# VectorE's order in a hybrid decoder trunk: residual adds ahead of waiting work, held banks later in the seventh part, values' low parts behind the softmax

## The chip, the cores and the metric

The kernel runs on one core of a Trainium2 chip. The metric is the time of one execution in microseconds (us). Its engines are named in the profile as PE (TensorE, matmuls), PEld (TensorE's weight loads, which overlap matmuls), DVE (VectorE), ACT (ScalarE), POOL (GpSimd) and SP (SyncE, which issues the loads).

## The reference

One sequence of 256 tokens with 2048 features goes through two layers. Layer 0 mixes tokens with a gated linear recurrence (RG-LRU), layer 1 with attention over 16 heads; each mixer is followed by an MLP with 8192 hidden features. All is float32.

```python
for i in range(DEPTH):                       # DEPTH = 2
    h = _rmsnorm(x, mix_norm[i])
    x = x + (_rglru_block(h, ...) if i % 2 == 0 else _dilated_attention_block(h, w_qkv, w_o))
    x = x + _mlp(_rmsnorm(x, mlp_norm[i]), mlp_w1[i], mlp_w2[i])
return _rmsnorm(x, final_norm)

def _mlp(h, w1, w2):                         # 2048 -> 8192 -> 2048
    return square(relu(h @ w1)) @ w2
```

## The kernel before

**Numbers in two halves.** Each operand of a matmul is split into a high part (rounded to `float32r`) and a low part, the rest. A product is then three matmuls: high by high, high by low, low by high. ScalarE rounds a weight tile of 128 x 2048 to its high part (`whi`, line 132) and VectorE subtracts to get the low part (`wlo`, line 136), one pair per tile that is loaded. The same split is made of the activations: `xT` is the scaled input turned round (line 218 its low half), `aT` the hidden features of the MLP, `sT` sums of them, `av` the values of the attention.

**Items and slots.** The whole program is a list of items. An item is TensorE's work on one weight tile. Around it the loop at the end writes the other engines' work in a fixed order, and each engine runs its own list strictly in that order: first the weight halves that are due (`before_unit`, two items ahead for `wlo`, three for `whi`), then the item itself, then all functions that were put down for this slot with `after(n, fn)` (n items later), then those put down with `at_end` (behind all others of the slot). Within a slot the functions of `after` stand in the order in which they were put down, but `att_p`, the transposes of a softmax, goes first.

**The residual.** It lies in four chunks `xc` of 512 features (`xc_68` to `xc_71` in the order's rows, chunk 0 to 3), each in two tiles of 128 tokens. When a product's bank in PSUM is complete, VectorE adds it to the residual: `add_x` (line 366) for plain products, `take` (line 686) in the MLPs. At the end of a stage `close_chunk` makes the function `done` for a chunk: it adds, takes square sums on ScalarE (line 270), and puts down `transpose_chunk` for the next slot, in which TensorE turns the chunk (line 242), ScalarE scales it into `xg` (245) and both make `xT` from it.

**The MLP.** It runs in eight parts, 0 to 7, of 1024 hidden features. In the parts 0 to 6 the second product is done for a pair of blocks by a scheme with seven products in place of eight (Strassen's, in Winograd's form): `b11`, `b21`, `t1`, `t2`, `b22`, `t3`, `t4`, once for the chunks 0 and 1 ("0" behind the name) and once for the chunks 2 and 3 ("1"). Between them lie eight items "w" of the first product of the part that follows. The order is a table:

```python
2: ("w", "b11 0", "t1 0", "w", "b21 0", "b22 0", "t2 0", "w", "t3 0", "w", "t4 0", "b11 1", "t1 1", "w",
    "b22 1", "t2 1", "w", "t3 1", "b21 1", "w", "w", "t4 1"),
HELD = {0: ("B", "T", "C"), 2: ("B",)}
```

Products gather in banks A, B, C and T. Those in `HELD` keep one of the four `acc` banks through the parts 0 to 6 and are added only in the seventh part (part 6). The others use the two `tr` banks in turn and are added right behind their product. The eight projections and the attention's scores use two `g` banks. In part 7 the second product is plain, and each chunk takes two `acc` banks.

**What follows an item "w".** `u_done` (line 592) scales it on VectorE into `uu`, ScalarE squares it and writes the high half of `aT`, and one slot later `u_low` (line 601) writes its low half on VectorE. Lines 612 to 625 make the sums `sT` from two such tiles; line 682 makes sums of weight tiles (`qT`).

**The attention.** Each head's scores go through `att_s`, `att_e` (exponentials, ScalarE, line 841), `att_n` (scaling, VectorE, lines 846 and 848, put down with `at_end`) and `att_p` (transposes, TensorE, line 853). `v_done` (lines 774 and 775) makes the two halves of the values `av` from two `acc` banks for four heads at a time.

Of the kernel before, what the change touches and what calls it, by code (L numbers as in the profile page):

```python
# [10 lines left out]
F32 = mybir.dt.float32  # L11
F32R = mybir.dt.float32r
AF = mybir.ActivationFunctionType
OP = mybir.AluOpType
# [55 lines left out]

HELD = {0: ("B", "T", "C"), 2: ("B",)}

TAKES = {"b11": 0, "b21": 0, "t1": 0, "t2": 0, "b22": 0, "t3": 0, "t4": 0}


@with_exitstack
def trunk(ctx: ExitStack, tc: tile.TileContext, a: dict, out: bass.AP):
    nc = tc.nc
# [14 lines left out]
    def form(load, make, source):  # L93

        units.append({"load": load, "make": make, "source": source})
        return len(units) - 1
# [69 lines left out]
    def item(u, fn, kind=None):  # L166
        items.append((u, fn, kind))

    later = {}
    now = [0]  # L170
# [20 lines left out]
    def after(n, fn, *args):  # L191
        later.setdefault(now[0] + n, []).append((fn, args))
# [3 lines left out]
    def at_end(fn, *args, **kwargs):  # L196

        ending.append((fn, args, kwargs))
# [15 lines left out]
    state = {}  # L214
# [5 lines left out]
    def new_xT(n):  # L220
        t = perm.tile([P, 4, 512], F32R, name=f"xT{n}")
        state["xT", n] = t
        return t
# [4 lines left out]
    def new_xg(n):  # L228
        if scope[0] in ("mlp", "end"):
            t = lru.tile([P, UW], F32, name=("q12", "q22")[n % 2])  # L230
            return t[:, 0:4 * S].rearrange("p (k s) -> p k s", k=4)
        return lru.tile([P, 4, S], F32, name="xg", bufs=2)
# [33 lines left out]
    def square_sum(n, ts=range(NT)):  # L266
        sq = state["ssq"]
        for t in ts:
            junk = perm.tile([P, 512], mybir.dt.bfloat16, name="junk")
            nc.scalar.activation(junk, xc[n][:, t, :], AF.Square, accum_out=sq[:, t, n:n + 1])  # L270

    def new_ssq():
        state["ssq"] = perm.tile([P, NT, NCH], F32, name="ssq", bufs=2)
# [64 lines left out]
    def three(bank, xh, xl, hi, lo, opens, closes, border):  # L338

        mm(bank, xh, in_turn(hi), opens, False)  # L340
        mm(bank, xh, in_turn(lo), False, False)
        cut = 256 if border else 512
        for at in range(0, 512, cut):
            mm(bank[:, at:at + cut], xl, in_turn(hi, at, cut), False, closes and at + cut == 512)
# [5 lines left out]
    def acc_tile():  # L350
        return psum.tile([P, 512], F32, name="acc", bufs=4)
# [12 lines left out]
    def add_x(n, acc):  # L364
        for t in range(NT):
            nc.vector.tensor_add(xc[n][:, t, :], xc[n][:, t, :], acc[t])

    def close_chunk(n, gname, rows):
        def done(acc):
            if n == 0:  # L370
                new_ssq()
            add_x(n, acc)
            if n < NCH - 1:
                square_sum(n)
            after(1, transpose_chunk, n, gname)
            if n == NCH - 1:
                after(1, square_sum, n)
                after(1, rstd_cols)
                if rows:
                    after(4, rstd_rows)  # L380
        return done

    def aT(j):
        return state["aT", j]
# [237 lines left out]
    def low_of_sums():  # L622
        if "low" in state:
            t, w = state.pop("low")
            nc.vector.tensor_sub(t[:, 4:8], w, t[:, 0:4].bitcast(F32))  # L625

    def standing(p, what):

        def get(k):
            if what[0] == "a":  # L630
                t, h = int(what[1]) - 1, int(what[2]) - 1
                x = aT(8 * (p % 2) + 4 * h + k)
                return x[:, t * 128:(t + 1) * 128], x[:, 256 + t * 128:256 + (t + 1) * 128]
            x = state["sT", p, k]
            return x[:, int(what[1])], x[:, 4 + int(what[1])]
        return get

    def plan_mlp(w1, w2, done):
# [26 lines left out]
        def plan_group(p, n0, last_group):  # L665


            q, bank = {}, held.setdefault(n0, {})
            ends = GROUPS[p + 1] < GROUPS[p]

            def fetch(name, h, n, tag):
                q[name] = (wts.tile([P, UW], F32, name="raw", bufs=RAW_BUFS) if tag == "raw"
                           else lru.tile([P, UW], F32, name=tag))
                nc.sync.dma_start(q[name], w2[((p // 2) * 4 + n0 + n) * 4 + (p % 2) * 2 + h])

            def add(to, a, b, by):
                if by == "dma":
                    nc.gpsimd.dma_start(q[to], q[b], accum_op=OP.add)
                    return
                if to not in q:  # L680
                    q[to] = lru.tile([P, UW], F32, name=to)
                nc.vector.tensor_add(q[to], q[a], q[b])  # L682

            def take(n, t, b, sign):
                x = xc[n0 + n][:, t, :]
                (nc.vector.tensor_add if sign > 0 else nc.vector.tensor_sub)(x, x, bank[b])  # L686

            def product(name, loads, source, what, b, first, takes):
                def load_all():
                    for l in loads:  # L690
                        fetch(*l)

                def make_all():
                    for m in SUMS.get(name, []):
                        add(*m)
                u = form(load_all, make_all, lambda: q[source])

                def run():
                    opens = first and (p == 0 or b not in HELD[n0])
                    if opens:  # L700
                        bank[b] = acc_tile() if b in HELD[n0] else psum.tile([P, 512], F32, name="tr", bufs=2)
                    hi, lo = split[u]
                    get = standing(p, what)
                    for k in range(4):
                        xh, xl = get(k)
                        s = slice(k * 512, (k + 1) * 512)
                        three(bank[b], xh, xl, hi[:, s], lo[:, s], opens and k == 0, k == 3,
                              state["border"] and k == 3)
                    for t in takes if ends or b not in HELD[n0] else ():
                        after(TAKES[name], take, *t)  # L710
                    if what == "s0" and last_group:
                        busy[0] = None
                    if what == "a11":
                        busy[0] = p
                item(u, run)

            table = (
                ("b11", [("b11", 0, 0, "raw")], "b11", "a11", "A", True, [(0, 0, "A", 1)]),
                ("b21", [("q21", 1, 0, "q21")], "q21", "a12", "B", True, [(0, 0, "B", 1)]),
                ("t1", [("q12", 0, 1, "q12")], "qT", "s3", *(  # L720
                    ("T", True, [(1, 1, "T", -1), (1, 0, "T", -1)]) if "T" in HELD[n0] else ("C", True, [(1, 1, "C", -1)]))),
                ("t2", [("q22", 1, 1, "q22")], "qT", "s1", "A", False, [(1, 0, "A", -1)]),
                ("b22", [], "q22", "s2", "C", "T" in HELD[n0], [(1, 0, "C", -1)]),
                ("t3", [], "q12", "s0", "A", False, [(1, 1, "A", -1)]),
                ("t4", [], "q21", "a22", "A", False, [(0, 1, "A", 1)]),
            )
            return {row[0]: (lambda row=row: product(*row)) for row in table}
# [29 lines left out]
    scale = HD ** -0.5  # L757
# [11 lines left out]
    def v_done(g, acc):  # L769
        v = lru.tile([P, 2, NT, 4, HD], F32R, name="av", bufs=2)  # L770
        att["v", g] = v
        for t in range(NT):
            col, x = state["rstd"][:, t:t + 1], acc[t].rearrange("p (h d) -> p h d", h=4)
            nc.scalar.activation(v[:, 0, t], x, AF.Copy, scale=col)
            nc.vector.scalar_tensor_tensor(v[:, 1, t], x, col, v[:, 0, t].bitcast(F32), op0=OP.mult, op1=OP.subtract)

    def qk_done(h, w, ps):
        y = lru.tile([P, S], F32, name="y", bufs=4)
# [287 lines left out]
    for n in range(NCH):  # L1066
        x = new_xg(n)
        t = new_xT(n)
# [18 lines left out]
        for what in order:  # L1087
            k = int(what[1])
            if what[0] == "w":
# [7 lines left out]
                                           op0=OP.mult, op1=OP.subtract)  # L1097
# [39 lines left out]
    for at, (u, fn, kind) in enumerate(items):  # L1137
        if u is None:
            fn()
            continue  # L1140
        before_unit(u)
        state["border"] = kind is None and at + 1 < len(items) and items[at + 1][2] == "w"
        fn()
        behind_unit(least[at] - 1)
        for f, args in sorted(later.pop(now[0], []), key=lambda e: e[0] is not att_p):
            f(*args)
        for f, args, kwargs in ending:
            f(*args, **kwargs)
        ending.clear()
        low_of_sums()  # L1150
        sums_of_tokens()
        if kind is None:
            sums_of_tokens()
        now[0] += 1
# [87 lines left out]
```

## Time and profile before

| | |
|---|---|
| time, median of 3 runs (lowest to highest) | 2021.68 us (2021.48 to 2022.02) |
| the profiled execution's own time | 2022.14 us |
| its span, first to last instruction | 2020.4 us |
| granted TensorE clock | 0.999 |
| busy: PE, PEld, DVE, ACT, POOL | 2006.2, 1876.2, 1724.6, 1293.7, 88.4 us |

A row of the order of time reads: start in us, length in us, engine, line, operation, output and input tiles, shape, count, and in brackets how long the engine stood idle before it and what ended that. A row of waits gives the engine and line that waited, on whom, the total in us, how often and the longest. A row of a group gives its count, busy time, mean ns of one, and idle time before. A row of windows gives the stretch, its length, the busy time of PE, PEld, DVE, ACT and POOL with instruction counts, the granted clock, the share of the DMA engines and GB/s.

Matmuls run at a regular step: a matmul of 512 columns starts 0.216 us after the one before, one of 256 columns 0.112.

### The profile page before, as it was taken

The numbers are of one execution on the slowest core, as the hardware profiler recorded it, in microseconds if no ns is written. First come the engines' busy times: TensorE is split into PE (matmuls) and PEld (weight loads), VectorE is DVE, ScalarE is ACT, GpSimd is POOL, SyncE is SP. The second block draws the span as 40 slices with busy tenths as digits, with TensorE's granted clock in tenths as the row PEclk, the third lists the DMA queues.
The fourth block names the chain that finished last, engine by engine and source line by source line (L and its number), as shares of the span: only waits on it lengthen the run. The fifth ranks groups of instructions, "written<-read, shape, count | busy, mean of one in ns | idle before, by whom it ended". The sixth has DMA issues, their size and how long they took to land.

```text
span 2020.4 us, 32932 instructions
## 1 busy us (share of the span) xinstructions
PE 2006.2 (99%) x13761; PEld 1876.2 (93%) x13761; DVE 1724.6 (85%) x1903; ACT 1293.7 (64%) x1420; POOL 88.4 (4%) x83
## 2 busy tenths in 40 slices
PE   9999999999999999999999999999999999999998
PEld 9999988999999999999889989889999999999997
DVE  7999865699999999998658959857999999999985
ACT  7878775566566666665657657656666666666664
POOL 0111110000000000000000000000000000000001
PEclk9999999999999999999999999999999999999999
DMA  8555565688787788777554555456787877887774
GB/s 310 204 195 201 183 229 190 246 252 250 258 284 264 230 292 270 248 238 255 197 214 175 186 188 179 176 193 245 250 250 264 283 265 228 297 270 248 233 260 153
DMA packets 68917, 472.54 MB, mean 234 GB/s; under 512 B 7584, under 2 KB 7712, under 8 KB 13472
## 3 DMA queue, kind: packets, MB, share of 16 engines
q1 hardware_dynamic: 60416, 411.18, 54.2%
q0 software_dynamic: 8064, 58.72, 14.6%
q8 instruction: 108, 1.77, 0.3%
q10 hardware_dynamic: 288, 0.52, 0.1%
q14 instruction: 41, 0.34, 0.0%
HBM read 409.58 MB, written 2.10 MB: 204 GB/s over the span
## 4 chain that ended last, share of the span: by engine, by line
PE 91%; DVE 6%; ACT 2%; issue 1%; DMA 0%; SPq 0%; DVEq 0%; ACTq 0%
PE acc L201 44%; PE g L201 29%; PE tr L201 17%; DVE wlo L136 3%; ACT whi L132 1%; DVE qT L682 1%; PE tr L242 0%; DVE xc L686 0%; DVE c L437 0%; PE tr L853 0%; DVE sT L625 0%; DVE uu L592 0%; DVE aT L601 0%; DMA par<-in_par 0%; DVE sw L612 0%
## 5 line engine op out<-in xcount | busy, mean ns | idle before, releaser
L132 ACT ACTIVATE whi<-raw 128x2048 fp32r<-128x2048 f32 (+1 forms) x309 | 568.9, 1845 | 317.1 <-PE acc L201 163.1
L136 DVE TENSOR_TENSOR wlo<-raw,whi 128x2048 fp32r<-128x2048 f32 (+1 forms) x309 | 678.1, 2197 | 96.7 <-ACT whi L132 96.3
L201 PE MATMUL g<-xT,whi 128*128 128x256 f32 x3649 | 617.1, 275 | 0.0
L201 PEld LDWEIGHTS g<-xT,whi 128*128 128x128 f32 x3649 | 553.9, 192 | 0.0
L201 PE MATMUL g<-xT,wlo 128*128 128x256 f32 x1824 | 503.0, 276 | 0.6 <-DVE wlo L136 0.4
L201 PE MATMUL acc<-xT,whi 128*128 128x256 f32 (+1 forms) x2212 | 456.3, 301 | 0.3 <-ACT whi L132 0.3
L201 PE MATMUL acc<-xT,wlo 128*128 128x256 f32 x1360 | 374.1, 275 | 0.6 <-DVE wlo L136 0.6
L201 PEld LDWEIGHTS acc<-xT,whi 128*128 128x128 f32 x2212 | 356.3, 192 | 14.4 <-ACT whi L132 1.2
L201 PEld LDWEIGHTS g<-xT,wlo 128*128 128x128 f32 x1824 | 350.1, 192 | 2.2 <-DVE wlo L136 1.1
L201 PE MATMUL acc<-whi,aT 128*128 128x512 f32 (+1 forms) x1086 | 322.9, 374 | 0.0
L136 DVE TENSOR_TENSOR wlo<-q,whi 128x2048 fp32r<-128x2048 f32 x112 | 255.8, 2284 | 23.5 <-ACT whi L132 23.2
L132 ACT ACTIVATE whi<-q 128x2048 fp32r<-128x2048 f32 x112 | 214.4, 1915 | 79.3 <-PE g L201 53.3
L201 PEld LDWEIGHTS acc<-xT,wlo 128*128 128x128 f32 x1360 | 261.9, 193 | 1.4 <-DVE wlo L136 1.3
L201 PEld LDWEIGHTS acc<-whi,aT 128*128 128x128 f32 x1086 | 204.0, 189 | 27.6
L201 PE MATMUL tr<-whi,sT 128*128 128x512 f32 (+1 forms) x728 | 212.8, 364 | 0.9
L201 PE MATMUL acc<-wlo,aT 128*128 128x512 f32 (+1 forms) x536 | 200.8, 376 | 0.0
L132 ACT ACTIVATE whi<-qT 128x2048 fp32r<-128x2048 f32 x56 | 107.6, 1922 | 127.5 <-PE g L201 93.0
L201 PEld LDWEIGHTS tr<-whi,sT 128*128 128x128 f32 x728 | 137.7, 189 | 24.1 <-issue 6.1
L201 PE MATMUL tr<-whi,aT 128*128 128x512 f32 (+1 forms) x462 | 140.3, 373 | 0.0
L136 DVE TENSOR_TENSOR wlo<-qT,whi 128x2048 fp32r<-128x2048 f32 x56 | 127.9, 2284 | 1.3 <-ACT whi L132 1.3
L201 PE MATMUL tr<-wlo,sT 128*128 128x512 f32 x336 | 127.3, 379 | 0.0
L201 PEld LDWEIGHTS acc<-wlo,aT 128*128 128x128 f32 x536 | 101.1, 189 | 13.2
(170 smaller groups left out, 2147.5 us busy)
## 6 DMA issues: line engine op xcount, KB each, us to landing
raw<-in_w SPq DMA_DIRECT2D x172, 1024.0 KB, 6.9
q<-in_w SPq DMA_DIRECT2D x84, 1024.0 KB, 8.0
raw<-in_w_in SPq DMA_DIRECT2D x35, 1024.0 KB, 4.8
raw<-in_w_qk SPq DMA_DIRECT2D x32, 1024.0 KB, 4.8
q<-q POOLq DMA_DIRECT2D x28, 1024.0 KB, 12.2
q<-qT POOLq DMA_DIRECT2D x28, 1024.0 KB, 7.5
raw<-in_w_out SPq DMA_DIRECT2D x20, 1024.0 KB, 4.8
raw<-in_w_v SPq DMA_DIRECT2D x16, 1024.0 KB, 4.8
```

The source lines that it names most:

```text
L132: nc.scalar.activation(split[i][0][:, s], r, AF.Copy)
L136: nc.vector.tensor_sub(split[i][1][:, s], r, split[i][0][:, s].bitcast(F32))
L201: nc.tensor.matmul(o, l, r, start=start, stop=stop, skip_group_check=True)
L682: nc.vector.tensor_add(q[to], q[a], q[b])
```

## The change

Three edits in the code that sets the order. `take` and `closed` (the new name of the function that `close_chunk` returns) now go first in their slot, like `att_p`. The adds of the held banks in part 6 are put down 12, 12, 18 and 3 items after their product, where it was 0; the 18 reaches the second item of part 7. `v_done` puts its two pairs of instructions down with `at_end`, so that they stand behind the softmax's scaling where both fall in one slot.

```diff
-TAKES = {"b11": 0, "b21": 0, "t1": 0, "t2": 0, "b22": 0, "t3": 0, "t4": 0}
+ENDS = {"t1 0": 12, "b21 0": 12, "b22 0": 18, "b21 1": 3}
...
     def close_chunk(n, gname, rows):
-        def done(acc):
+        def closed(acc):
...
-        return done
+        return closed
...
-                        after(TAKES[name], take, *t)
+                        after(ENDS[f"{name} {n0 // 2}"] if b in HELD[n0] else 0, take, *t)
...
         for t in range(NT):
-            col, x = state["rstd"][:, t:t + 1], acc[t].rearrange("p (h d) -> p h d", h=4)
-            nc.scalar.activation(v[:, 0, t], x, AF.Copy, scale=col)
-            nc.vector.scalar_tensor_tensor(v[:, 1, t], x, col, v[:, 0, t].bitcast(F32), op0=OP.mult, op1=OP.subtract)
+            at_end(v_part, v, t, state["rstd"][:, t:t + 1], acc[t].rearrange("p (h d) -> p h d", h=4))
+
+    def v_part(v, t, col, x):
+        nc.scalar.activation(v[:, 0, t], x, AF.Copy, scale=col)
+        nc.vector.scalar_tensor_tensor(v[:, 1, t], x, col, v[:, 0, t].bitcast(F32), op0=OP.mult, op1=OP.subtract)
...
-        for f, args in sorted(later.pop(now[0], []), key=lambda e: e[0] is not att_p):
+        for f, args in sorted(later.pop(now[0], []), key=lambda e: e[0].__name__ not in ("att_p", "take", "closed")):
```

TensorE, GpSimd and SyncE run the same instructions in the same order as before. ScalarE's order differs in two places, where two square sums (line 270) of chunk 1 now stand ahead of `xg` and `xT` of chunk 0. The rest is VectorE's. The function that closes a chunk at the end of the last MLP (`final_done`) keeps its name and its place. New lines behind the diff's first edit are numbered 2 higher where the function lies behind `v_done`.

VectorE in part 0 of the first MLP, behind the items `t3 0` (first pair of rows that moves) and `t4 0` (second pair); `aT` is `u_low`'s, `xc` with `tr` a `take`. Before:

```order
L682 TENSOR_TENSOR qT<-raw,q_4749 128x2048
L601 TENSOR_TENSOR aT_4808<-uu,aT_4808 128x256
L686 TENSOR_TENSOR xc_69<-xc_69,tr 128x512
L136 TENSOR_TENSOR wlo<-raw,whi 128x2048
L592 SCALAR_TENSOR_TENSOR uu<-g,rstdB 128x256
L136 TENSOR_TENSOR wlo<-qT,whi 128x2048
L601 TENSOR_TENSOR aT_4888<-uu,aT_4888 128x256
L686 TENSOR_TENSOR xc_68<-xc_68,tr 128x512
L136 TENSOR_TENSOR wlo<-raw,whi 128x2048
```

VectorE at the same place now:

```order
L682 TENSOR_TENSOR qT<-raw,q_4749 128x2048
L686 TENSOR_TENSOR xc_69<-xc_69,tr 128x512
L601 TENSOR_TENSOR aT_4808<-uu,aT_4808 128x256
L136 TENSOR_TENSOR wlo<-raw,whi 128x2048
L592 SCALAR_TENSOR_TENSOR uu<-g,rstdB 128x256
L136 TENSOR_TENSOR wlo<-qT,whi 128x2048
L686 TENSOR_TENSOR xc_68<-xc_68,tr 128x512
L601 TENSOR_TENSOR aT_4888<-uu,aT_4888 128x256
L136 TENSOR_TENSOR wlo<-raw,whi 128x2048
```

The two neighbours change places; there are 84 such pairs in the two MLPs, six per part.

VectorE in part 6 of the first MLP, behind the items `t1 0`, `b21 0` and `b22 0`, whose held banks (`acc`) it adds. Before:

```order
L682 TENSOR_TENSOR qT<-qT,q_9288 128x2048
L686 TENSOR_TENSOR xc_69<-xc_69,acc 128x512 x2
L136 TENSOR_TENSOR wlo<-q_9288,whi 128x2048
L592 SCALAR_TENSOR_TENSOR uu<-g,rstdB 128x256
L136 TENSOR_TENSOR wlo<-qT,whi 128x2048
L601 TENSOR_TENSOR aT_9387<-uu,aT_9387 128x256
L686 TENSOR_TENSOR xc_68<-xc_68,acc 128x512
L136 TENSOR_TENSOR wlo<-raw,whi 128x2048
L686 TENSOR_TENSOR xc_69<-xc_69,acc 128x512
L136 TENSOR_TENSOR wlo<-q_9079,whi 128x2048
```

VectorE now has three of these four adds behind `b22 1` (first two) and behind the "w" that is two items on, in the same part:

```order
L136 TENSOR_TENSOR wlo<-raw,whi 128x2048
L686 TENSOR_TENSOR xc_69<-xc_69,acc 128x512 x2
L686 TENSOR_TENSOR xc_71<-xc_71,tr 128x512
L601 TENSOR_TENSOR aT_9702<-uu,aT_9702 128x256
L136 TENSOR_TENSOR wlo<-q_9442,whi 128x2048
L686 TENSOR_TENSOR xc_71<-xc_71,tr 128x512
L136 TENSOR_TENSOR wlo<-q_9644,whi 128x2048
L686 TENSOR_TENSOR xc_68<-xc_68,acc 128x512
L592 SCALAR_TENSOR_TENSOR uu<-g,rstdB 128x256
```

The fourth (`b22 0`, `xc_69`) went to part 7, ahead of the adds that close chunk 0, and the add of `b21 1` (`xc_70`) moved three items back, to the end of part 6.

VectorE in the attention, in the one slot where values (`av`) and a softmax's scaling (`m`, `s`) meet. Before:

```order
L881 TENSOR_TENSOR o<-o,g 128x256
L775 SCALAR_TENSOR_TENSOR av<-acc,rs,av 128x512 x2
L1148 TENSOR_TENSOR aT_11811<-o,aT_11811 128x256
L846 RECIPROCAL m<-m 128x2
L848 TENSOR_SCALAR s<-s,m 128x128
L848 TENSOR_SCALAR s<-s,m 128x256
L136 TENSOR_TENSOR wlo<-raw,whi 128x2048 x2
```

VectorE at the same place now:

```order
L883 TENSOR_TENSOR o<-o,g 128x256
L1150 TENSOR_TENSOR aT_11811<-o,aT_11811 128x256
L848 RECIPROCAL m<-m 128x2
L850 TENSOR_SCALAR s<-s,m 128x128
L850 TENSOR_SCALAR s<-s,m 128x256
L777 SCALAR_TENSOR_TENSOR av<-acc,rs,av 128x512 x2
L136 TENSOR_TENSOR wlo<-raw,whi 128x2048 x2
```

The values' low parts went from ahead of the scaling to behind it. In two more places, at the ends of the recurrent block and of the attention, the two adds of chunk 1 (line 366) now stand ahead of the two low halves of chunk 0's `xT` (line 218).

## The prediction

> **What bounds the kernel now.** I read the page first: TensorE is busy 99% of the span, so only its pauses can be won. Then the waits of TensorE and of its weight loads, then the instructions in order of time around each pause.
>
> ```profile
> PE 2006.2 (99%) x13761; PEld 1876.2 (93%) x13761; DVE 1724.6 (85%) x1903; ACT 1293.7 (64%) x1420; POOL 88.4 (4%) x83
> PE acc L201 <- DVE wlo L136: 1.6, 3, 0.6
> PEld tr L201 <- issue: 6.1, 14, 0.4
> ```
>
> The second and third row are waits: total us, times, longest. The third is the largest: fourteen weight loads of bank `tr` start 0.44 us late (6.1/14) with no releaser named. It is one per part of the two MLPs. Busy time hides pauses, since a matmul that starts late is still drawn with its length, so I measure a pause between the starts of matmuls. The first of the fourteen on TensorE:
>
> ```profile
> 441.58 0.59 PE L201 MATMUL tr<-whi,aT 128*128 128x512 f32 x2
> 443.95 0.38 PE L201 MATMUL tr<-wlo,aT 128*128 128x512 f32 x1
> 444.17 0.38 PE L201 MATMUL tr<-whi,aT 128*128 128x512 f32 x1
> 444.61 0.45 PE L201 MATMUL tr<-whi,sT 128*128 128x512 f32 x1
> 444.90 0.38 PE L201 MATMUL tr<-wlo,sT 128*128 128x512 f32 x1
> ```
>
> The regular step is 0.22 us (443.95 to 444.17; 0.216 over long runs). From 444.17 to 444.90 two steps took 0.73 in place of 0.43: the pause costs 0.30 us. The matmul at 444.61 is the first of product `t1 1` and opens a `tr` bank. There are two such banks; `b11 1`, just before it, took one, and the other was last filled by `t4 0`, whose last matmul starts at 441.58. So `t1 1` waits until VectorE has added that bank. VectorE there:
>
> ```profile
> 443.45 0.42 DVE L601 TENSOR_TENSOR aT<-uu,aT 128x256 fp32r<-128x256 f32 x1
> 443.79 0.68 DVE L686 TENSOR_TENSOR xc<-xc,tr 128x512 f32<-128x512 f32 x1
> ```
>
> The add ends at 444.47 and TensorE starts 0.14 later, at 444.61. It stood behind `aT` (`u_low`), which nobody needs yet.
>
> **Part 1: adds ahead of `u_low` in the MLP parts.** Six pairs per part change places in the MLPs, 84 in all; no instruction is added or removed, and no order on TensorE, GpSimd or SyncE changes. With the add first it starts at 443.45, ends at 444.13, and releases TensorE at about 444.27 by the same 0.14. TensorE would want the bank at 444.17 + 0.22 = 444.39. So the pause vanishes with 0.12 us to spare: 14 x 0.30 = 4.2 us. The other 70 pairs win nothing, since TensorE does not wait there. What could be lost is the wait of an add for its own product:
>
> ```profile
> L686 DVE TENSOR_TENSOR xc<-xc,tr 128x512 f32<-128x512 f32 x140 | 95.0, 678 | 0.0
> ```
>
> Busy 95.0 us, 678 ns each, idle before 0.0: in all 140, VectorE never waited in front of an add, its bank was long complete. An add drawn 0.34 earlier is unlikely to change that (`t4 0` ended about 1.5 us before its add). `u_low` comes 0.60 later; its readers are the products of the next part, and TensorE's next item in each case reads older tiles. The weight halves (`wlo`) behind the pair start when they did, since the pair's sum is the same. Cost 0; if that cover went, a pair would cost at most the add's 0.68.
>
> **Part 2: held banks in the seventh part.** The adds of `t1 0`, `b21 0` and `b22 0` stand in the middle of a stretch where TensorE waits for `wlo`:
>
> ```profile
> 896.30 1.28 DVE L686 TENSOR_TENSOR xc<-xc,acc 128x512 f32<-128x512 f32 x2
> 897.49 2.28 DVE L136 TENSOR_TENSOR wlo<-q,whi 128x2048 fp32r<-128x2048 f32 x1
> 902.57 0.68 DVE L686 TENSOR_TENSOR xc<-xc,acc 128x512 f32<-128x512 f32 x1
> ```
>
> ```profile
> 898.93 0.38 PE L201 MATMUL acc<-whi,sT 128*128 128x512 f32 x1
> 899.83 0.48 PE L201 MATMUL acc<-wlo,sT 128*128 128x512 f32 x1 [0.53 <-DVE wlo L136]
> 900.15 0.38 PE L201 MATMUL acc<-whi,sT 128*128 128x512 f32 x1
> 904.90 0.39 PE L201 MATMUL g<-xT,whi 128*128 128x256 f32 x2
> 905.71 0.39 PE L201 MATMUL g<-xT,whi 128*128 128x256 f32 x2
> 1908.92 0.48 PE L201 MATMUL acc<-wlo,sT 128*128 128x512 f32 x1 [0.53 <-DVE wlo L136]
> ```
>
> 898.93 to 900.15 is 1.22 for two steps of 0.216: 0.79 lost. 904.90 to 905.71 holds three matmuls of half width (0.11 each): 0.81 - 0.33 = 0.48 lost. The last row is the same wait in the second MLP, so 2 x 1.27 = 2.5 us. Without the double add `wlo` runs from 896.30 to 898.58 and is there before 899.15, when it is wanted; the second gains 1.28 + 0.68, more than its 0.48. The adds go back in later: 1.28 at `b22 1` and 0.68 two items on, ahead of this:
>
> ```profile
> 942.89 0.42 DVE L592 SCALAR_TENSOR_TENSOR uu<-g,rstdB 128x256 f32<-128x256 f32 x1 [0.43 <-PE g L201]
> 944.72 2.29 DVE L136 TENSOR_TENSOR wlo<-raw,whi 128x2048 fp32r<-128x2048 f32 x1 [1.41 <-ACT whi L132]
> ```
>
> 1.96 us against 0.43 + 1.41 = 1.84 us of idle time: what follows comes some 0.1 late. TensorE's projection that uses this `wlo` starts at 948.04, one microsecond after it is written (947.01):
>
> ```profile
> 948.04 10.72 PE g L201 x96
> ```
>
> I take 0; the bound is that all of it shows, 2 x 1.96 = 3.9. The last add (`b22 0`) now comes two items into the eighth part, in front of the second pair of accumulators, which gets its bank only then: a new wait of TensorE, between 0 and one add (0.68) per MLP. I take 0, since its place is in VectorE's idle time.
>
> **Part 3: values' low parts behind the softmax.** In one place `av` stood before the softmax's scaling, for which the transposes wait. The same place without it (first two rows) and with it:
>
> ```profile
> 1155.66 0.38 PE L201 MATMUL acc<-whi,xT 128*128 128x512 f32 x1
> 1156.13 0.80 PE L201 MATMUL g<-pT,av 128*128 128x256 f32 x5
> 1167.47 0.38 PE L201 MATMUL acc<-whi,xT 128*128 128x512 f32 x1
> 1169.11 0.80 PE L201 MATMUL g<-pT,av 128*128 128x256 f32 x5
> ```
>
> ```profile
> 1165.66 0.19 ACT L841 ACTIVATION_READ_ACCUMULATOR s<-s,m 128x1 f32 x1
> 1166.46 1.41 DVE L775 SCALAR_TENSOR_TENSOR av<-acc,rs,av 128x512 fp32r<-128x512 f32 x2 [4.27 <-ACT av L774]
> 1168.31 0.55 DVE L848 TENSOR_SCALAR s<-s,m 128x128 f32<-128x128 f32 x2
> ```
>
> 0.47 against 1.64: 1.17 us lost. The exponentials are done at 1165.85, VectorE is idle then, and the scaling would end near 1166.7, before TensorE comes at 1167.7. All 1.2 us are won. `av` and the two `wlo` behind it end no later than before.
>
> **Part 4: `closed` ahead of the transposes' low halves.** At two borders (recurrent block, attention) chunk 1 is added behind chunk 0's `xT` halves, and TensorE's transposes of chunk 1 wait for the add:
>
> ```profile
> 302.81 0.38 PE L201 MATMUL acc<-whi,aT 128*128 128x512 f32 x1
> 303.82 0.46 PE L201 MATMUL acc<-whi,aT 128*128 128x512 f32 x1
> 308.87 0.38 PE L201 MATMUL acc<-whi,aT 128*128 128x512 f32 x1
> 310.43 0.46 PE L201 MATMUL acc<-whi,aT 128*128 128x512 f32 x1
> 1328.54 0.38 PE L201 MATMUL acc<-whi,aT 128*128 128x512 f32 x1
> 1330.10 0.46 PE L201 MATMUL acc<-whi,aT 128*128 128x512 f32 x1
> ```
>
> ```profile
> 305.05 1.55 ACT L245 ACTIVATE xg<-tr,par 128x256 f32<-128x256 f32 x4
> 307.15 1.29 DVE L218 TENSOR_TENSOR xT<-xg,xT 128x512 fp32r<-128x512 f32 x2 [4.86 <-ACT xT L217]
> 308.36 1.28 DVE L366 TENSOR_TENSOR xc<-xc,acc 128x512 f32<-128x512 f32 x2
> ```
>
> Eight transposes undisturbed take 1.01 us from the matmul before to the one behind, here 1.56 and 1.56: 2 x 0.55 = 1.1 us. Ahead of `xT` the adds would run when their banks are done, about 303 to 304.2, five microseconds early. In exchange ScalarE does two square sums before `xg`, some 1.5 us; `xg`, which empties the transposes' banks, ends near 308.1 and not 306.6, still before 309.09, when they are refilled.
>
> **The sum.** 4.2 + 2.5 + 1.2 + 1.1 = 9.0 us off the profiled execution's own 2022.14 (its span 2020.4): 2013.1. The median of the runs is 2021.68, 0.46 lower, so 2012.7. The bounds: each pause is at least not longer than now (gain 0) and goes wholly (9.0); I take the upper ends, since each freed instruction comes ahead of its need by the rows.
>
> One rule would make the sum larger. The Trainium skill, TensorE: Matmul & The Clock Gate, "A second HAM failure mode", says that short idles between groups of matmuls that cycle through PSUM banks can let the clock gate fall back, so that each pause would cost more than itself. By it the 14 pauses would each be followed by slowed matmuls. The trace has none: the granted clock (column before the last two) is 1.00 across such pauses, so nothing more is to be won.
>
> ```profile
> 450.00:530.00 80.00, 79.94 (x565) 75.21 (x564) 75.55 (x69) 50.78 (x43) 3.42 (x4) 1.00 0.81 266
> ```
>
> **Rivals.** (a) The fourteen pauses stay or return later in the part: the margin is 0.12 us only, and VectorE is busy 75.5 of 80 us (third busy column of that row), so TensorE's lead might be lost at the next `wlo`. Against it: VectorE idles 0.43 and 1.41 us later in each part, waiting for TensorE's end, and so moves with it. Time 2021.7 - 4.8 = 2016.9. (b) The held adds take their 2.5 us back where they now stand: 2015.2. (c) Both: 2019.4, within 0.2%. (d) Slower: an add placed first waits for its own product, and VectorE's order makes all `wlo` behind it wait. A part has 80 - 75.5 = 4.5 us to spare; six such waits of w use it up at w = 0.75, and the loss exceeds the gain of 9.0 (0.64 a part) from w = 0.86. At w = 1.1 it is 14 x (6.6 - 4.5) - 9.0 = +20: 2042. Against it stands the idle 0.0 of the L686 row.
>
> The Trainium skill speaks for (d): PSUM — Partial Sum Buffer, "Engine vs sequencer instructions", states that VectorE's queue is strictly first in, first out, so whatever stands behind a waiting add waits too. The trace agrees on the order, but shows no waiting add.
>
> **How the numbers follow.** All four parts win, 2012.7: 0.71, its own range 2011.2 to 2014.3 (some tenths for each added wait, and the runs' 0.3). (a) 0.11, (b) 0.08, (c) 0.06, (d) 0.04. Less than 4.04 us (0.2%, about what a measurement of this kernel can tell) is only in (c) and (d): faster 0.90, same 0.06, slower 0.04. The range runs from 2011.0 to (a) with the runs' spread, 2017.2, and leaves out (c) and (d).
>
> **What would show it.** Right: no weight load of `tr` with "issue" 0.4 before it, or nearly none; no wait for `wlo` near 899 and 905; 0.47 and 1.01 us in the rows of parts 3 and 4; L686 still idle 0.0 before it; span near 2011.4. Wrong: rows of `wlo` with new waits of TensorE around 936 to 948 or at the eighth part's second pair of accumulators; L686 with idle time ended by PE; pauses of `t1 1` moved but not gone.

## The result, and the profile after

The changed kernel takes 2015.26 us (median of 6 runs, 2014.45 to 2015.86), the kernel before 2021.86 (6 runs, 2021.48 to 2022.71). The ratio is 0.9966, 95% interval 0.9956 to 0.9977: 6.9 us faster, 4.6 to 8.9. The forecast was 2012.7, with a range of 2011.0 to 2017.2. The sign and three of the four terms hold; the largest term, part 1, came out half as large. The profiled execution has a span of 2013.1 us (before 2020.4) and took 2014.87.

The page after, first the busy times, then the group of the adds of the `tr` banks. Then, from the list of TensorE's waits, those for weight halves:

```profile
PE 2001.9 (99%) x13761; PEld 1876.5 (93%) x13761; DVE 1721.5 (86%) x1903; ACT 1294.2 (64%) x1420; POOL 87.9 (4%) x83
...
L686 DVE TENSOR_TENSOR xc<-xc,tr 128x512 f32<-128x512 f32 x140 | 95.1, 680 | 0.0
```

```profile
PE acc L201 <- DVE wlo L136: 0.6, 2, 0.3
PE g L201 <- DVE wlo L136: 0.2, 1, 0.2
```

VectorE still never waits in front of an add (0.0 in the last column). TensorE's longest wait for a `wlo` is 0.3 us (0.6 before), and no wait for the softmax's `s` is left in its list. In the list of the weight loads the row "PEld tr L201 <- issue: 6.1, 14, 0.4" has no successor.

These lists say which waits went, not what was won. That is read by laying the starts of the same matmul in both traces side by side. The rows after, in order of time; the rows before them in the prediction are the partners:

```profile
303.39 0.46 PE L201 MATMUL acc<-whi,aT 128*128 128x512 f32 x1
...
309.44 0.46 PE L201 MATMUL acc<-whi,aT 128*128 128x512 f32 x1
...
443.19 0.38 PE L201 MATMUL tr<-whi,aT 128*128 128x512 f32 x1
443.40 0.38 PE L201 MATMUL tr<-whi,sT 128*128 128x512 f32 x1
443.62 0.38 PE L201 MATMUL tr<-wlo,sT 128*128 128x512 f32 x1
...
897.09 0.38 PE L201 MATMUL acc<-whi,sT 128*128 128x512 f32 x1
897.52 0.38 PE L201 MATMUL acc<-whi,sT 128*128 128x512 f32 x1
902.61 0.39 PE L201 MATMUL g<-xT,whi 128*128 128x256 f32 x2
...
1164.21 0.38 PE L201 MATMUL acc<-whi,xT 128*128 128x512 f32 x1
1164.67 0.80 PE L201 MATMUL g<-pT,av 128*128 128x256 f32 x5
...
1325.11 0.46 PE L201 MATMUL acc<-whi,aT 128*128 128x512 f32 x1
1902.36 0.38 PE L201 MATMUL acc<-wlo,sT 128*128 128x512 f32 x1
```

| matmul | start before | start after | lead | what was won since the row above |
|---|---|---|---|---|
| behind the first transposes | 303.82 | 303.39 | 0.43 | start-up, not the change (below) |
| behind chunk 1's transposes | 310.43 | 309.44 | 0.99 | part 4: 0.56 |
| last of `b11 1` | 444.17 | 443.19 | 0.98 | - |
| second of `t1 1` | 444.90 | 443.62 | 1.28 | part 1: 0.30 |
| `t1 0` of part 6, first | 898.93 | 897.09 | 1.84 | 0.56: five more pauses of `t1 1` gone, and not 5 x 0.30 |
| the same, third | 900.15 | 897.52 | 2.63 | part 2: 0.79 |
| the next "w" | 905.71 | 902.61 | 3.10 | part 2: 0.47 |
| attention, last projection | 1167.47 | 1164.21 | 3.26 | the seventh pause, net 0.16 |
| attention, behind the transposes | 1169.11 | 1164.67 | 4.44 | part 3: 1.18 |
| end of the attention | 1330.10 | 1325.11 | 4.99 | part 4: 0.55 |
| second MLP, part 6 | 1908.92 | 1902.36 | 6.56 | six pauses, and the first half of part 2 |

Everything stands where it was expected, with one exception: after each `t1 1` something is given back. It is found 8 us later, at the first matmul of `b22 1`. Before, then after:

```profile
452.53 0.28 PE L201 MATMUL g<-xT,wlo 128*128 128x256 f32 x1
452.64 0.38 PE L201 MATMUL tr<-whi,sT 128*128 128x512 f32 x1
452.86 0.38 PE L201 MATMUL tr<-wlo,sT 128*128 128x512 f32 x1
```

```profile
451.25 0.28 PE L201 MATMUL g<-xT,wlo 128*128 128x256 f32 x1
451.43 0.45 PE L201 MATMUL tr<-whi,sT 128*128 128x512 f32 x1
451.72 0.38 PE L201 MATMUL tr<-wlo,sT 128*128 128x512 f32 x1
451.94 0.38 PE L201 MATMUL tr<-whi,sT 128*128 128x512 f32 x1
```

Before, the starts are 0.11 and 0.22 apart, the regular steps. Now they are 0.18 and 0.29 apart, and then 0.22 again: 0.07 of waiting, and 0.075 more for the step behind it, 0.15 together, in each of the 14 parts. The list of waits does not show it, and TensorE counts as busy throughout; the one mark of it in the rows is the bar at 451.43, drawn 0.45 long in place of 0.38. VectorE there, before and after, the latter from `t4 0`'s add on:

```profile
451.59 0.67 DVE L686 TENSOR_TENSOR xc<-xc,tr 128x512 f32<-128x512 f32 x1
```

```profile
442.47 0.68 DVE L686 TENSOR_TENSOR xc<-xc,tr 128x512 f32<-128x512 f32 x1
443.06 0.42 DVE L601 TENSOR_TENSOR aT<-uu,aT 128x256 fp32r<-128x256 f32 x1
443.40 2.28 DVE L136 TENSOR_TENSOR wlo<-raw,whi 128x2048 fp32r<-128x2048 f32 x1
...
447.80 0.68 DVE L686 TENSOR_TENSOR xc<-xc,tr 128x512 f32<-128x512 f32 x1
448.40 2.28 DVE L136 TENSOR_TENSOR wlo<-q,whi 128x2048 fp32r<-128x2048 f32 x1
450.60 0.68 DVE L686 TENSOR_TENSOR xc<-xc,tr 128x512 f32<-128x512 f32 x1
```

The add at 450.60 is that of `t1 1`, which gathers in a `tr` bank (bank C for these chunks). `b22 1` goes on gathering in the same bank (its row in the table has `"T" in HELD[n0]` as "first", which is false for the chunks 2 and 3), so it may start only when `t1 1`'s add has read it: 451.28, and 0.15 later TensorE starts, at 451.43. Before, the add ended at 452.26, some 0.23 (0.38 less 0.15) ahead of what the matmul at 452.64 needed. Now the add starts 0.99 earlier (450.60 for 451.59), which is the lead that the kernel had before `t1 1` (0.98 in the table); TensorE has 0.30 more than that, and the add does not: `u_low` stands one place later, but still ahead of it. 0.30 - 0.23 = 0.07 of waiting.

That is theory T. Rival R1 is (a) of the prediction: the lead is lost to a weight half (`wlo`), as this whole stretch of VectorE is nearly full. R2 is that the add has no part in it: what is missing is scatter of the start-up (in the first runs below), or the pause has some other cause, such as the change of the bank (in the last ones).

### The profile page after: what moved, and what is told of

It is laid out like the page before. It is cut to its first block, busy times and chain, and to the rows that moved or that the text cites. A ratio compares the mean times of both kernels' runs of the same rounds, so it can differ in the third digit from the quotient of the medians.

```text
span 2013.1 us, 32932 instructions
## 1 busy us (share of the span) xinstructions
PE 2001.9 (99%) x13761; PEld 1876.5 (93%) x13761; DVE 1721.5 (86%) x1903; ACT 1294.2 (64%) x1420; POOL 87.9 (4%) x83
## 4 chain that ended last, share of the span: by engine, by line
PE 96%; DVE 3%; ACT 0%; issue 0%; DMA 0%; SPq 0%; ACTq 0%
PE acc L201 46%; PE g L201 32%; PE tr L201 18%; DVE wlo L136 1%; PE tr L242 1%; DVE c L437 0%; DMA raw<-in_w_first 0%; ACT whi L132 0%; PE tr L855 0%; DVE c L433 0%; DVE sT L625 0%; DVE qT L682 0%; DVE gw L462 0%; ACT xc L973 0%; DVE i L515 0%
## 5 line engine op out<-in xcount | busy, mean ns | idle before, releaser
L201 PE MATMUL g<-xT,whi 128*128 128x256 f32 x3649 | 617.0, 275 | 0.0
L201 PEld LDWEIGHTS g<-xT,whi 128*128 128x128 f32 x3649 | 554.0, 192 | 0.0
L201 PE MATMUL g<-xT,wlo 128*128 128x256 f32 x1824 | 502.9, 276 | 0.2 <-DVE wlo L136 0.2
L201 PE MATMUL acc<-xT,whi 128*128 128x256 f32 (+1 forms) x2212 | 455.3, 300 | 0.7 <-ACT whi L132 0.7
L201 PE MATMUL acc<-xT,wlo 128*128 128x256 f32 x1360 | 373.3, 274 | 0.7 <-DVE wlo L136 0.6
L201 PEld LDWEIGHTS acc<-xT,whi 128*128 128x128 f32 x2212 | 355.5, 191 | 15.1 <-ACT whi L132 1.8
L201 PEld LDWEIGHTS g<-xT,wlo 128*128 128x128 f32 x1824 | 350.1, 192 | 1.5 <-DVE wlo L136 0.4
L201 PE MATMUL acc<-whi,aT 128*128 128x512 f32 (+1 forms) x1086 | 322.9, 374 | 0.0
L201 PEld LDWEIGHTS acc<-xT,wlo 128*128 128x128 f32 x1360 | 261.1, 192 | 1.6 <-DVE wlo L136 1.5
L201 PEld LDWEIGHTS acc<-whi,aT 128*128 128x128 f32 x1086 | 204.0, 189 | 27.6
L201 PE MATMUL tr<-whi,sT 128*128 128x512 f32 (+1 forms) x728 | 212.7, 364 | 0.0
L201 PE MATMUL acc<-wlo,aT 128*128 128x512 f32 (+1 forms) x536 | 200.8, 376 | 0.0
L201 PEld LDWEIGHTS tr<-whi,sT 128*128 128x128 f32 x728 | 137.6, 189 | 20.5
L201 PE MATMUL tr<-whi,aT 128*128 128x512 f32 (+1 forms) x462 | 140.3, 373 | 0.0
L201 PE MATMUL tr<-wlo,sT 128*128 128x512 f32 x336 | 127.4, 379 | 0.0
L201 PEld LDWEIGHTS acc<-wlo,aT 128*128 128x128 f32 x536 | 101.1, 189 | 13.2
```

Source lines behind the costliest of these rows:

```text
L201: nc.tensor.matmul(o, l, r, start=start, stop=stop, skip_group_check=True)
```

## The experiments

Eight kernels were run, the first four of the table in one session and the last four in another, each beside runs of the kernel before (2021.79 us in the median in the first, 2022.48 in the second). The start-up, the first 80 us, differs from execution to execution, and with it the start of all that follows. The matmul behind the first transposes, earliest (e3) and latest (e7):

```profile
302.87 0.46 PE L201 MATMUL acc<-whi,aT 128*128 128x512 f32 x1
304.94 0.46 PE L201 MATMUL acc<-whi,aT 128*128 128x512 f32 x1
```

So beside the time the table has the span from this matmul on: the span, less its start. For the kernel before it is 2020.4 - 303.82 = 1716.6, for the changed one 2013.1 - 303.39 = 1709.7.

| run | median us (lowest to highest) | ratio to before, 95% interval | span less start | against |
|---|---|---|---|---|
| e1_adds_first | 2019.45 (2018.96 to 2020.06) | 0.9989, 0.9980 to 0.9998 | 2017.7 - 303.31 = 1714.4 | before -2.2 |
| e2_held_late | 2019.36 (2018.55 to 2020.50) | 0.9988, 0.9979 to 0.9997 | 2017.3 - 303.35 = 1714.0 | before -2.6 |
| e3_values_closed | 2019.11 (2018.60 to 2020.64) | 0.9989, 0.9980 to 0.9997 | 2017.1 - 302.87 = 1714.2 | before -2.4 |
| e6_only_t4 | 2014.72 (2014.61 to 2015.18) | 0.9966, 0.9952 to 0.9979 | 2012.8 - 303.26 = 1709.5 | changed -0.2 |
| e4_ulow_later | 2013.04 (2012.84 to 2014.37) | 0.9955, 0.9943 to 0.9968 | 2011.2 - 303.72 = 1707.5 | changed -2.2 |
| e5_add_before_wlo | 2012.66 (2012.19 to 2014.13) | 0.9953, 0.9940 to 0.9965 | 2010.9 - 303.41 = 1707.5 | changed -2.2 |
| e7_double | 2019.59 (2018.88 to 2020.97) | 0.9986, 0.9977 to 0.9995 | 2019.0 - 304.94 = 1714.1 | changed +4.4 |
| e8_two_ulow | 2011.19 (2010.51 to 2011.27) | 0.9943, 0.9931 to 0.9956 | 2009.2 - 303.80 = 1705.4 | changed -4.3 |

Differences "by the medians" to the changed kernel are taken to its 2015.26. It was not run beside these eight. The intervals of e4 to e6 overlap its own (0.9956 to 0.9977), those of e7 and e8 touch it. So what the last five runs show rests on their rows, laid beside its rows matmul by matmul; the times only agree with them.

### Each part alone

**e1_adds_first.** The kernel before with the one key:

```diff
-        for f, args in sorted(later.pop(now[0], []), key=lambda e: e[0] is not att_p):
+        for f, args in sorted(later.pop(now[0], []), key=lambda e: e[0].__name__ not in ("att_p", "take")):
```

> The kernel before with part 1 alone (take goes first in its slot). Theory T: TensorE wins 0.30 us at the first matmul of t1 1 in each of 14 parts, but loses 0.15 again 8 us later, at the first matmul of b22 1, which waits for the add of t1 1's bank; that add stands where it stood, since u_low ahead of it only changed places with the add before. 14 x 0.15 = 2.1 us faster, 2019.8. Rival R1 (VectorE's whole stretch is the bound, the lead is lost at the next wlo): the same total, but the second pause ends with a wlo and stands at another matmul. Rival R2 (the term was right, the shortfall is the start-up or scatter): 4.2 us faster, 2017.7, no pause at b22 1.

Measured: 2.3 us faster by the medians, 2.2 by the span. The interval (0.4 to 4.0 us) leaves out R2's 4.2. TensorE, at `b22 1` of the first part:

```profile
451.72 0.28 PE L201 MATMUL g<-xT,wlo 128*128 128x256 f32 x1
451.90 0.46 PE L201 MATMUL tr<-whi,sT 128*128 128x512 f32 x1
452.20 0.38 PE L201 MATMUL tr<-wlo,sT 128*128 128x512 f32 x1
```

0.18 and 0.30: the pause belongs to part 1 alone and is not an effect of the parts together. The place is the product's first matmul, which reads `whi`; the wait on a `wlo` that R1 needs would stand at the second.

**e2_held_late.** The kernel before with the table `ENDS` and its use:

```diff
-                        after(TAKES[name], take, *t)
+                        after(ENDS[f"{name} {n0 // 2}"] if b in HELD[n0] else 0, take, *t)
```

> The kernel before with part 2 alone (held banks added 12, 12, 18 and 3 items later). All theories: 2 x 1.25 = 2.5 us faster, 2019.4; no matmul near 942 to 970 pays it back. If the adds that moved cost something that another part of the change hides: less than 2.5.

Measured: 2.4 by the medians, 2.6 by the span. As forecast; the adds that moved pay nothing back, and they don't need another part's cover.

**e3_values_closed.** The changed kernel with the old `TAKES` and without `take` in the key:

```diff
+        for f, args in sorted(later.pop(now[0], []), key=lambda e: e[0].__name__ not in ("att_p", "closed")):
```

> The kernel before with parts 3 and 4 alone (values' low parts behind the softmax, chunk 1's adds ahead of the low halves of chunk 0). All theories: 1.2 + 2 x 0.55 = 2.3 us faster, 2019.6; three places in the trace, nothing else. With the two runs beside it theory T gives 2.1 + 2.5 + 2.3 = 6.9 for the sum, R2 gives 9.0.

Measured: 2.7 by the medians, 2.4 by the span. The three add to 2.3 + 2.4 + 2.7 = 7.4 by the medians and 7.2 by the spans, beside 6.6 and 6.9 for the whole change. The parts are independent to within the scatter, and the sum is T's 6.9, not 9.0.

**e6_only_t4.** The changed kernel, in which only the adds of `t4 0` carry a name that goes first:

```diff
+            def take_t4(*t):
+                take(*t)
...
+                        after(ENDS[...] if b in HELD[n0] else 0, take_t4 if name == "t4" and n0 == 0 else take, *t)
...
+        for f, args in sorted(later.pop(now[0], []), key=lambda e: e[0].__name__ not in ("att_p", "take_t4", "closed")):
```

> The changed kernel, but of the 84 pairs only the 14 behind the item t4 0 change places; the other 70 stand as before the change. Theory T and the prediction's step on the 70 pairs: the same as the changed kernel, 2015.0 within 0.4 us. If some of the 70 carry a part of the gain (or of the loss at b22 1): slower (or faster) than it by up to 2 us.

Measured: the same. Laid side by side, no step of TensorE behind the start-up differs by more than 0.04 us, and the pause at `b22 1` is there in all 14 parts. The other 70 pairs neither win nor lose, and the pause is no doing of theirs.

### What `b22 1` waits for

**e4_ulow_later.** Item `j` = 5 of the first product is the "w" ahead of `t4 0`:

```diff
-        after(1, u_low, t, uu)
+        after(3 if p and j == 5 else 1, u_low, t, uu)
```

> The changed kernel, and in each of 14 parts the one u_low that stands between the adds of t4 0 and t1 1 goes two items later, behind the add of t1 1. That add then starts 0.34 us earlier (the step that one u_low of 0.42 takes in VectorE's row). Theory T (b22 1 waits for that add): the 0.15 at b22 1 goes, 14 x 0.15 = 2.1 us faster than the changed kernel's 2015.0: 2012.9. Rival R1 (the lead is lost to the weight halves behind): since each wlo between also comes 0.34 earlier, the same or a pause at the wlo of t2 1 instead, 2012.9 to 2015.0. R2 (the pause comes from something else, such as the bank change itself): 2015.0, the 0.15 stays.

Measured: 2.2 us less than the changed kernel by both the medians and the span. TensorE and VectorE in the first part:

```profile
451.58 0.28 PE L201 MATMUL g<-xT,wlo 128*128 128x256 f32 x1
451.69 0.38 PE L201 MATMUL tr<-whi,sT 128*128 128x512 f32 x1
451.91 0.38 PE L201 MATMUL tr<-wlo,sT 128*128 128x512 f32 x1
```

```profile
450.60 0.68 DVE L686 TENSOR_TENSOR xc<-xc,tr 128x512 f32<-128x512 f32 x1
451.20 0.41 DVE L601 TENSOR_TENSOR aT<-uu,aT 128x256 fp32r<-128x256 f32 x1
```

Regular steps again, 0.11 and 0.22. The add starts at 450.60 as in the changed kernel, but TensorE is 0.33 later here, from the start-up; beside TensorE it is earlier by that much. R2 is out. R1 is not yet, as the weight halves moved as well.

**e5_add_before_wlo.** In the slot of `t1 1` the last weight half waits until the slot's functions are written (`late` holds these items):

```diff
-        step("lo", min(i + 1 + LOOK_LO, ROWS + 2 if "rows" in state else len(units)), cut_lo)
+        step("lo", min(i + LOOK_LO + (i not in late), ROWS + 2 if "rows" in state else len(units)), cut_lo)
...
             f(*args)
+        if u in late:
+            late.remove(u)
+            before_unit(u)
```

> The changed kernel, and the add of t1 1 goes ahead of the wlo that stood before it, which is b22 1's own: the add comes 2.2 us earlier, that wlo 0.6 later, all behind it where it was. Tells T from R1. T: the wlo ends at 451.28 in the first part, with 0.14 at 451.42, and TensorE wants it with b22 1's second matmul at 451.57; the pause goes, 2.1 us faster: 2012.9. R1 (weight halves set the pace): the wait on wlo grows by up to 0.6 a part, 2015.0 to 2023.4. R2: 2015.0.

Measured: 2.2 us less by the span, 2.6 by the medians. VectorE, then TensorE (line numbers one higher):

```profile
447.82 1.27 DVE L687 TENSOR_TENSOR xc<-xc,tr 128x512 f32<-128x512 f32 x2
449.02 2.28 DVE L136 TENSOR_TENSOR wlo<-q,whi 128x2048 fp32r<-128x2048 f32 x1
```

```profile
451.26 0.28 PE L202 MATMUL g<-xT,wlo 128*128 128x256 f32 x1
451.38 0.38 PE L202 MATMUL tr<-whi,sT 128*128 128x512 f32 x1
451.59 0.38 PE L202 MATMUL tr<-wlo,sT 128*128 128x512 f32 x1
```

The weight half is 0.62 later (449.02 for 448.40), the add 2.2 earlier, and the pause is gone in all 14 parts. A weight half that sets the pace could not be put off for nothing: R1 is out. It is just in time: it ends at 451.30, and the matmul that reads it starts at 451.59.

**e7_double.** The suspected delay, doubled:

```diff
         after(1, u_low, t, uu)
+        if p and j == 5:
+            after(3, again, t, uu)
...
+    def again(t, uu):
+        u_low(t, uu)
```

`again` also goes first in its slot, so it stands right ahead of `t1 1`'s add.

> The changed kernel with one more instruction per part: the u_low of e4 is done where it stood, and once more (the same values into the same place) right ahead of the add of t1 1, 0.34 us. T: each of the 14 pauses at b22 1 grows from 0.15 to 0.49, 4.8 us slower: 2019.8, no other pause. R1: t2 1's wlo is late too and the pauses there add to it: over 2020. R2 (TensorE does not wait for this add): 2015.0.

Measured: 4.4 us more than the changed kernel by the span, 4.3 by the medians. Now the list of TensorE's waits names the cause itself, and the rows show it (line numbers are five higher on VectorE):

```profile
PE tr L201 <- DVE xc L691: 3.4, 14, 0.2
```

```profile
452.16 0.41 DVE L606 TENSOR_TENSOR aT<-uu,aT 128x256 fp32r<-128x256 f32 x1
452.49 0.68 DVE L691 TENSOR_TENSOR xc<-xc,tr 128x512 f32<-128x512 f32 x1
```

```profile
452.79 0.28 PE L201 MATMUL g<-xT,wlo 128*128 128x256 f32 x1
453.31 0.45 PE L201 MATMUL tr<-whi,sT 128*128 128x512 f32 x1 [0.25 <-DVE xc L691]
453.61 0.38 PE L201 MATMUL tr<-wlo,sT 128*128 128x512 f32 x1
```

Fourteen waits for `xc` of `take`'s line, where the changed kernel's list has none. From 452.79 to 453.61 two steps take 0.82 in place of 0.33: 0.49 lost, T's number. The list counts 0.25 of them, since a bar's end covers part and the slow second step is not in it. Laid side by side, each of the 14 pauses grew by 0.33 to 0.34; 14 of these make 4.6, and one pause at another place, near 730 us in the changed kernel, is 0.25 shorter here (why is not shown), which leaves the 4.4. T is shown: `b22 1` waits for `t1 1`'s add, and the 0.15 is what `u_low` ahead of that add costs.

**e8_two_ulow.** The same remedy at the next place where TensorE waits. In the changed kernel it still pauses 0.18 in the fourth item of a part, whose `wlo` comes late; there the `u_low` of the part's last "w" (`j` = 7) stands in front:

```diff
-        after(1, u_low, t, uu)
+        after(3 if p and j == 5 or j == 7 and 0 < p < 7 else 1, u_low, t, uu)
```

> e4, and in twelve parts the u_low of the last item w two items later as well, behind the wlo of the fourth item, where TensorE still pauses for that wlo in the changed kernel (0.19 us, in one place 0.43). Theory T: both pauses go, 2.1 + 12 x 0.19 + 0.24 = 4.6 us faster than the changed kernel: 2010.4. If the second pause is set by ScalarE's half or by a load: only 2.1, 2012.9. If VectorE's stretch is the bound all along (R1), the lead is lost at the next wait: 2013 to 2015.

Measured: 2011.19, 4.1 less than the changed kernel by the medians and 4.3 by the span, a ratio of 0.9943 to before: the fastest of all ten kernels. TensorE at that place in the changed kernel, then here:

```profile
491.10 0.39 PE L201 MATMUL g<-xT,whi 128*128 128x256 f32 x2
491.40 0.38 PE L201 MATMUL g<-xT,wlo 128*128 128x256 f32 x1
491.61 0.39 PE L201 MATMUL g<-xT,whi 128*128 128x256 f32 x2
```

```profile
491.37 0.39 PE L201 MATMUL g<-xT,whi 128*128 128x256 f32 x2
491.60 0.28 PE L201 MATMUL g<-xT,wlo 128*128 128x256 f32 x1
491.71 0.39 PE L201 MATMUL g<-xT,whi 128*128 128x256 f32 x2
```

Three matmuls took 0.51 and now take 0.34. Both pauses yield to the same move. The forecast was 4.6 less. Laid side by side, the pauses at `b22 1` are gone in all 14 parts, and those in the fourth item in eleven of twelve, 0.18 each and not 0.19. The twelfth, the long one, falls from 0.42 to 0.07, and a new one of 0.10 stands 13 us behind it. Together that is 2.1 + 2.0 + 0.35 - 0.1, the 4.3 by the span.

## Why the prediction was right, and where not

- **Part 1 (4.2 forecast, 2.1 measured): the step that failed.** The mechanism at `t1 1` is as written: the add of `t4 0` starts at 442.47, ends at 443.15, and TensorE opens the bank at 443.40 without a pause, 14 times 0.30. What failed is that the whole 0.30 was taken as won, by the sentence "The other 70 pairs win nothing, since TensorE does not wait there". It is true of the pairs (e6), but it was taken for all that follows. TensorE did not wait at `b22 1` because it came 0.30 late; its margin there was 0.23. The prediction asked for each margin at the place of the pause (0.12, and about that much was left) and not for those of the next waits on the same stretch of VectorE, which moves no earlier. Its reason against a returning pause was VectorE's idle time later in the part. That idle time lies behind `b22 1`: in the changed kernel's first part VectorE's first wait behind `t4 0`'s add is one of 0.30 for TensorE, before the instruction at 462.25. Between the two it has no idle time to give.
- **The size of what came back.** Margin 0.23, lead 0.30, so 0.07 of lateness; with the 0.075 that the next step takes longer it is 0.15, half of the gain.
- **Part 2 (2.5; 2 x 1.26 measured, e2 2.4 to 2.6).** Right by place and size. The moved adds wait for nothing and delay nothing: between 902.61 and 1164.21 the lead grows by 0.16, which is one more part's net gain.
- **Part 3 (1.2; 1.18).** Right: 1164.67 - 1164.21 is 0.46, beside 0.47 at the undisturbed place.
- **Part 4 (1.1; 0.56 + 0.55).** Right.
- **The sum.** 2.1 + 2.5 + 1.2 + 1.1 = 6.9; the profiled spans differ by 7.3, of which 0.43 is the start-up. The prediction's 9.0 stands just outside the measured interval. Its time of 2012.7 is 2.6 us below the median, 2.1 of them by part 1; the range holds the median because it reached as far as (a).
- **Rival (a)** came nearest to what happened: a pause that returns later in the part, 2016.9 for a full loss. It looked for it at the next `wlo`, where e5 shows 0.6 us to spare; it was an add. The time of (b), 2015.2, is the measured one almost to the digit, but by chance: (b) has the held adds lose their 2.5 us, and e2 keeps them. (c) falls with e2 as well. (d) falls with the 0.0 in front of the 140 adds.
- **The signs.** All that the prediction named as a sign of being right is there, but for the span (2013.1 for 2011.4): the weight loads' row is gone from the list while half of what it promised was lost again at another matmul. A wait that leaves a list is not yet time won.
- **The clock.** The prediction weighed whether each short pause would slow the matmuls behind it. The trace: behind a pause one step is 0.075 longer and the next is regular (451.43, 451.72, 451.94); the granted clock over the stretch is 1.00:

```profile
450.00:530.00 80.00, 80.00 (x566) 75.46 (x565) 75.69 (x69) 50.40 (x42) 3.42 (x4) 1.00 0.82 266
```

## What to carry to other kernels

When an engine's pause is taken away, everything behind it comes earlier by the pause, and each later wait on a partner that does not move along, and whose margin is smaller, gives back the difference. So list, behind the pause, the next places where that engine needs the same partner, with the margin of each (wanted less ready): of the pause no more survives than the smallest of these margins, here 0.23 less the 0.075 of the new stop, 0.15 of 0.30. Of two instructions on a nearly full engine, it is not enough to swap the pair: the one that nobody needs has to go behind the last one that is waited for.

## What was not expected of the hardware

- A matmul that has waited cost more than its wait here: the step behind it is 0.29 in place of 0.216 us, in the 0.07 pauses of the changed kernel (451.43 to 451.72), in the 0.41 ones of e7 (453.31 to 453.61) and in those before (444.61 to 444.90). So a wait of 0.07 costs 0.15. With 256 columns the step is 0.21 in place of 0.112 (491.40 to 491.61 in the changed kernel). The reason is not shown, and a late start is not needed for it: in e8 a matmul that starts on time at 742.38 has a step of 0.21 as well.
- From the drawn end of VectorE's add to the start of the matmul that waited for it are 0.15 us (451.28 to 451.43) and 0.14 in e7 (453.17 to 453.31). The Trainium skill, Perfetto Trace Analysis, "DVE / Act Engine Instruction", has the release of a semaphore reach the other engines only after the end that the profiler reports. These rows agree.
- The start-up differs by up to 2.1 us between the ten profiled executions (302.87 to 304.94 for the same matmul), as much as part 1's net gain. From there on the profiles agree better: the three parts' spans add to 7.2 beside 6.9 for the whole.
